# Attention scores: the low parts of the keys kept twice over, so that the second score product contracts 128 rows

## The chip, the cores and the metric

The kernel runs on one core of one Trainium2 chip. The metric is the device time of one launch in microseconds; before the change the median of three runs is 2069.76 us (2068.32 to 2070.65).

## What is computed

The reference is a network for one sequence of 512 tokens and a width of 1024, all in float32. A first block joins a pooling mixer with an attention of 8 heads of 64 columns over blocks of 256 keys (below: moba) and has a large MLP. A second block has two layers: one with differential attention (8 heads, each with two score maps of 64 columns; below: diff), one with windowed attention (16 query heads, 4 key heads, 64 columns; below: swa), each followed by a gated MLP with a small convolution. What bears on the change is the product that makes the scores, which all three attentions have:

```python
s_own = jnp.einsum('bhqd,bhkd->bhqk', qc, k_own) - slope * dist[None, None]      # moba
...
s = jnp.einsum('bqhd,bkhd->bhqk', qb, k).astype(jnp.float32) * scale             # diff
...
s = jnp.einsum('bnqhgd,bnchd->bnhgqc', q, kb).astype(jnp.float32) * (d ** -0.5)  # swa
```

## The kernel before, in words

TensorE multiplies in the type `float32r`, which keeps fewer bits than float32. Every operand is therefore held as a high part and a low part (`split`, line 75: ScalarE writes the high part, VectorE what is left over), and a linear layer makes three products of each pair of 128x128 weights and 128x512 activations (`mm3`, line 102: high by high at line 105, low by high at 106, high by low at 107). The weights come through `wst` (two buffers, loaded from SyncE's queue), and are split into `whi` and `wlo` (four buffers each, lines 93, 91 and 94).

Scores have a contraction of 64 only. Two heads (or the two maps of a diff head) share a tile of 128 partitions, head m = 0 in partitions 0 to 63 and m = 1 in 64 to 127. `stack_q` (line 810) rearranges a query tile by three copies so that each of the two heads has a full tile, with high parts in one half and low parts in the other. `stack_k` (line 817) likewise makes two tiles from the keys' high parts, each holding one head's high part twice. All these copies are DMAs from SBUF to SBUF on SyncE's queue. The score of a query block is then made by two products (`dots`, line 823): step 0 (line 827) contracts 128 rows, [query high; query low] with [key high; key high]; step 1 (line 830) contracts only the 64 partitions of head m, query high with key low, straight from the tile of the keys' low parts (`qkl` in moba, `dl` in diff, `kl` in swa). The query is the stationary operand, the keys stream.

In the program of a query block (`scores`, lines 585, 909 and 1095) these two products are followed by others into the same bank: in moba from the third query block on by one that contracts 2 rows (line 601, the gate's mask), and always by one for the distance (line 603); in swa by one for the band (line 1121); in diff by none, and there steps 0 of both maps are written down before steps 1 of both. The result is read by VectorE (a maximum: lines 605, 929 and 1123), ScalarE takes the exponential, and two to five query blocks later TensorE turns the weights (`flip`) and multiplies them with the values (`values`).

Attention is woven into linear work (`weave`, line 154): the generator `lin` makes queries, keys, values and part of the next projection, `att` the query blocks, and a table of stages and microseconds says how much linear work stands ahead of each block. A scheduler then orders the instructions of each engine when the program is built; at run time each engine works through its own order and waits on semaphores.

Of the kernel before, what the change touches and what calls it, by code (L numbers as in the profile page):

```python
# [15 lines left out]
S = 512  # L16
D = 1024
# [12 lines left out]
def f32(ap):  # L30
    return ap.bitcast(F32)


class Net:
# [16 lines left out]
    # ---------------------------------------------------------------- helpers  # L51
    def mm_ps(self, shape=(128, S)):
        """a bank for a linear layer's output: outside attention its banks are shared out too"""
        banks = (("mm", 2), ("sc", 2), ("mm", 2), ("sc", 2), ("pv", 1))[:self.wide]
        self.bank = (self.bank + 1) % len(banks)
        tag, bufs = banks[self.bank]
        return self.ps.tile(list(shape), F32, name=tag, tag=tag, bufs=bufs)
# [17 lines left out]
    def split(self, src, hi, lo, scale=None):  # L75
        """hi + lo = src (* scale)"""
# [32 lines left out]
    def tiles(self, w, k0, kt, cols):  # L109
        """weight tiles [128, kt, 128] (hi, lo) for the column starts in cols, loaded two at a time"""  # L110
# [12 lines left out]
    def linear_steps(self, w, x, cols, evac, k0=0, group=1, order=None, ready=None, first=None, ahead=(), hold=None):  # L123
        """a linear layer as a generator that yields after each k tile: ns of tensor time, or a mark it waits for;
        group output tiles (first, the first ones) take their k tiles in turn"""
# [28 lines left out]
    def weave(self, att, lin, pace):  # L154
        """attention chunks with linear work between them: pace gives (stage, us of linear work behind it by then)"""
# [4 lines left out]
        def advance():  # L160
            """one step of the linear work; None if it waits for a mark or has ended"""
# [43 lines left out]
    # -------------------------------------------------------------- constants  # L205
# [33 lines left out]
    def load_cols(self, names, rows):  # L239
        """per-channel columns of the rows of names"""  # L240
# [11 lines left out]
    def late_consts(self):  # L252
        nc, a = self.nc, self.a
        # rotary tables
# [36 lines left out]
    def conv_cols(self, rows):  # L291
        """conv columns: taps 0..2 and the bias, tile by tile"""
# [6 lines left out]
    # ------------------------------------------------------------------ norms  # L299
    def rsqrt(self, x, y, tmp):  # L300
        """y = x ** -0.5 for narrow tiles"""
# [7 lines left out]
    def col_stats(self, acc, which):  # L309
        """token-column sums [128, NT] of a feature-major tile, times the constant in self.ones"""  # L310
# [6 lines left out]
    def bcast(self, col):  # L317
        """[128, S] in PSUM, every partition the row of the token columns col [128, NT]"""
# [19 lines left out]
    def rstd(self, wide=True):  # L338
        """the token columns rstd [128, NT] and, wide, their broadcast over partitions [128, S]"""
# [13 lines left out]
    def later(self, f):  # L353
        """f's result, computed where it is first asked for"""
# [12 lines left out]
    def pre(self, n, src, gain, gi, fast=False):  # L367
        """squares and the gained split of tile n of the next layer's input"""
# [6 lines left out]
    # --------------------------------------------------------------- block one  # L375
    def load_x(self):
        """x, turned feature-major, with the first layer's first tiles on its heels"""
# [131 lines left out]
    def v_steps(self, w, c0, Rcol, dst, x):  # L509
        """token-major values: dst(t) -> (hi, lo) APs [128, 256] for the 256 columns from c0"""  # L510
# [14 lines left out]
    def moba(self, win, R, Rcol, P):  # L525
# [25 lines left out]
        def qk(i):  # L551
            def evac(n, ps):
# [3 lines left out]
                lo = P.tile([128, S], F32R, name="qkl%d" % n, tag="qkl%d" % n, bufs=2)  # L556
                self.split(f, hi, lo, 0.125 if n == 0 else None)
                sw = self.stacked(4 + i % 2 * 2 + n)
                QK[i, n] = (f, hi, sw, lo)
                if n == 0:  # L560
                    self.stack_q(hi, sw, lo)
                else:
                    self.stack_k(hi, sw)
# [10 lines left out]
        def gate(i):  # L574
            g = self.st_ps((2, 256))
            nc.tensor.matmul(g, QK[i, 2], QK[i, 0][0][:, 256:], start=True, stop=True)
            mr = P.tile([2, 256], F32, name="mr", tag="mr", bufs=2)
            nc.vector.tensor_scalar(mr, g, 0.125 / 256, NEG, op0=OP.mult, op1=OP.is_lt)
            mk = P.tile([2, 256], F32R, name="mk", tag="mk", bufs=2)
# [32 lines left out]
        def flip(h, t):  # L612
            """key block b, query block t of the transposed weights lies at 3 b + t"""
# [154 lines left out]
    def post(self, y, h, gain, gi, meanwhile):  # L768
        """the next layer's input from h + y * rstd of one operand, gained already, which ends in self.h"""
# [8 lines left out]
    # --------------------------------------------------------------- block two  # L778
    def rope(self, P, ps, cosR, sinR, hi, lo, scale=None):
        """split of the rotated tile: x * cos + swap(x) * sin, with the norm's rstd in the tables"""  # L780
# [12 lines left out]
    def spill(self):  # L793
        """h to DRAM: attention takes its tiles"""
# [14 lines left out]
    def stack_q(self, a, b, lo):  # L809
        """a = [hi 0; hi 1], lo = [lo 0; lo 1] -> a = [hi 0; lo 0], b = [lo 1; hi 1]"""  # L810
# [5 lines left out]
    def stack_k(self, a, b):  # L816
        """a = [hi 0; hi 1] -> a = [hi 0; hi 0], b = [hi 1; hi 1]"""
# [3 lines left out]
        nc.sync.dma_start(f32(a[64:, :]), f32(a[:64, :]))  # L821

    def dots(self, ps, q, k, m, qs, ks, step, last=False):
        """one of two products that make queries' dots with keys, of half m of the stacked tiles"""
        nc = self.nc
        if step == 0:
            nc.tensor.matmul(ps, q[m][:, qs], k[m][:, ks], start=True, stop=False)  # L827
        else:
            pp = slice(64 * m, 64 * m + 64)
            nc.tensor.matmul(ps, q[m][pp, qs], k[2][pp, ks], start=False, stop=last)  # L830

    def pv(self, ps, v, ph, pl, ps0, ph0, first, last):
        """values of 64 columns: v is [hi lo], and ps gets hi's products in its upper half, lo's in its lower;
        the first covers the bank"""
# [6 lines left out]
    def halves(self, P, ps, hi, lo):  # L841
        """split of the sum of the halves of pv's product"""
# [4 lines left out]
    def tables(self, P, R):  # L847
        nc = self.nc
        """the rotary tables times rstd; the sine's takes the place of R"""
# [9 lines left out]
    def diff(self):  # L859
# [4 lines left out]
        with tc.tile_pool(name="diff", bufs=1) as P:  # L864
# [31 lines left out]
            def qk(h):  # L896
                def evac(n, ps):
                    e = h % 2 * 4 + 2 * n
                    hi, sw = self.stacked(e), self.stacked(e + 1)
                    lo = P.tile([128, S], F32R, name="dl%d" % n, tag="dl%d" % n, bufs=2)  # L900
# [3 lines left out]
                    else:  # L904
                        self.stack_k(hi, sw)
# [565 lines left out]
```

## Time and profile before

| | |
|---|---|
| three runs | 2068.32, 2069.76, 2070.65 us |
| span of the profiled execution | 2068.3 us |
| TensorE (PE) busy | 2029.0 us, 98% |
| VectorE (DVE) busy | 1271.2 us, 61% |
| ScalarE (ACT) busy | 799.0 us, 39% |
| GpSimd (POOL) busy | 444.3 us, 21% |
| mean granted TensorE clock | 0.996 of 2.4 GHz |
| line 830 (the 64-row products) | 160 products: 32 in moba, 64 in diff, 64 in swa |
| moba's scores | from about 140 to 238 us of the span |
| diff's scores | from about 797 to 981 us |
| swa's scores | from about 1478 to 1598 us |

The profiled execution has no time of its own beside its span; the span equals the shortest of the three runs and lies 1.5 us under their median. In the trace a matmul's record begins when it starts and ends after its pipeline has drained, so the records of a dense stream overlap; what a product costs the stream is the distance from its start to the start of the next, not its duration. `PEld` is the load of the stationary operand, `SPq` SyncE's queue of DMA issues. A line such as `64*128 64x512` reads: 64 rows by 128 columns of the array used, a streamed operand of 64 partitions by 512 columns.

### The profile page before, as it was taken

Reading aid. Unit: us, or ns where it says so; the run is one execution under the profiler, and the core shown is the slowest. Engines: PE = TensorE matmul, PEld = TensorE weight load, DVE = VectorE, ACT = ScalarE, POOL = GpSimd, SP = SyncE. Lnnn points to the kernel's source line nnn. Section 1 sums busy time; section 2 is a strip of 40 time slices with the busy share of each in tenths; the row PEclk is TensorE's granted clock in tenths of the full one; section 3 lists DMA queues with packets and bytes.
Section 4 is the critical chain, followed back from the end, with each engine's and each line's share of the span. In section 5 each row is a group of like instructions: output and inputs, shape, how many; then the busy total and the mean of one; then the engine's idle time right before and its main releaser. Section 6 shows DMA issues by size and latency. Waiting matters only on the chain.

```text
span 2068.3 us, 25392 instructions
## 1 busy us (share of the span) xinstructions
PE 2029.0 (98%) x9426; PEld 1625.9 (79%) x9426; DVE 1271.2 (61%) x2038; ACT 799.0 (39%) x1388; POOL 444.3 (21%) x514
## 2 busy tenths in 40 slices
PE   8999999899999989999999999999999999999997
PEld 7887787787888877777788888887877788888886
DVE  6456655723444487778675465667688675465665
ACT  4324434422222354555343231334466343332342
POOL 5011224100000231110221113132234221113122
PEclk9999999999999999999999999999999999999999
DMA  5342344232332355433232332334532232334331
GB/s 195 98 139 57 100 147 138 90 102 82 102 102 93 111 159 139 110 90 103 83 88 94 107 101 84 92 127 143 145 92 70 82 102 88 96 102 126 88 102 61
DMA packets 260493, 218.82 MB, mean 106 GB/s; under 512 B 9285, under 2 KB 235666, under 8 KB 260370
## 3 DMA queue, kind: packets, MB, share of 16 engines
q1 hardware_dynamic: 256746, 211.90, 34.3%
q10 hardware_dynamic: 3624, 5.31, 0.8%
q8 instruction: 74, 1.21, 0.2%
q14 instruction: 49, 0.40, 0.1%
HBM read 182.83 MB, written 14.16 MB: 95 GB/s over the span
## 4 chain that ended last, share of the span: by engine, by line
PE 91%; DVE 6%; issue 1%; ACT 1%; DMA 1%; POOL 0%; SPq 0%; ACTq 0%; POOLq 0%; DVEq 0%
PE mm L105 12%; PE mm L107 12%; PE mm L106 12%; PE sc L106 10%; PE sc L107 10%; PE sc L105 10%; PE pv L105 5%; PE pv L107 5%; PE pv L106 5%; PE sc L830 3%; PE sc L827 2%; PE pv L839 1%; DVE ul L83 1%; PE tr L1148 1%; PE sc L1121 1%
## 5 line engine op out<-in xcount | busy, mean ns | idle before, releaser
L94 DVE TENSOR_TENSOR wlo<-wst,whi 128x1024 fp32r<-128x1024 f32 (+2 forms) x304 | 393.8, 1298 | 200.1 <-ACT whi L93 143.7
L93 ACT ACTIVATE whi<-wst 128x1024 fp32r<-128x1024 f32 (+2 forms) x203 | 207.2, 1025 | 459.6 <-PE sc L106 181.3
L106 PE MATMUL mm<-ul,whi 128*128 128x512 f32 x704 | 278.1, 395 | 11.5 <-DVE ul L83 11.5
L105 PE MATMUL mm<-uh,whi 128*128 128x512 f32 x704 | 281.4, 400 | 0.4 <-ACT uh L82 0.4
L107 PE MATMUL mm<-uh,wlo 128*128 128x512 f32 x704 | 276.7, 393 | 0.0
L91 POOL TENSOR_SCALAR whi<-wst 128x1024 fp32r<-128x1024 f32 (+2 forms) x101 | 108.0, 1069 | 734.0 <-PE mm L106 231.7
L105 PE MATMUL sc<-uh,whi 128*128 128x512 f32 x496 | 194.9, 393 | 0.0
L106 PE MATMUL sc<-ul,whi 128*128 128x512 f32 x496 | 194.3, 392 | 0.2 <-DVE ul L83 0.2
L107 PE MATMUL sc<-uh,wlo 128*128 128x512 f32 x496 | 194.2, 392 | 0.0
L106 PEld LDWEIGHTS mm<-ul,whi 128*128 128x128 f32 x704 | 132.8, 189 | 41.9 <-DVE ul L83 18.1
L105 PEld LDWEIGHTS mm<-uh,whi 128*128 128x128 f32 x704 | 132.7, 189 | 28.3 <-issue 3.5
L107 PEld LDWEIGHTS mm<-uh,wlo 128*128 128x128 f32 x704 | 132.5, 188 | 28.3 <-issue 1.7
L107 PEld LDWEIGHTS sc<-uh,wlo 128*128 128x128 f32 x496 | 93.5, 189 | 20.6 <-DVE wlo L94 0.7
L105 PEld LDWEIGHTS sc<-uh,whi 128*128 128x128 f32 x496 | 93.6, 189 | 19.6 <-issue 0.4
L106 PEld LDWEIGHTS sc<-ul,whi 128*128 128x128 f32 x496 | 93.6, 189 | 19.3 <-DVE ul L83 0.5
L105 PE MATMUL sc<-ah,whi 128*128 128x512 f32 x264 | 104.4, 396 | 0.0
L106 PE MATMUL sc<-al,whi 128*128 128x512 f32 x264 | 104.3, 395 | 0.0
L107 PE MATMUL sc<-ah,wlo 128*128 128x512 f32 x264 | 104.2, 395 | 0.0
L105 PE MATMUL pv<-uh,whi 128*128 128x512 f32 x256 | 100.7, 393 | 0.0
L107 PE MATMUL pv<-uh,wlo 128*128 128x512 f32 x256 | 100.6, 393 | 0.0
L106 PE MATMUL pv<-ul,whi 128*128 128x512 f32 x256 | 100.2, 391 | 0.0
L1233 ACT ACTIVATE cv<-cu,cc 128x512 f32<-128x512 f32 x88 | 71.0, 813 | 60.3 <-DVE cu L1231 60.2
(455 smaller groups left out, 4343.5 us busy)
## 6 DMA issues: line engine op xcount, KB each, us to landing
wst<-ffn_w_up SPq DMA_DIRECT2D x88, 512.0 KB
wst<-w_up SPq DMA_DIRECT2D x16, 1024.0 KB
wst<-w_down SPq DMA_DIRECT2D x16, 1024.0 KB
wst<-ffn_w_down SPq DMA_DIRECT2D x16, 1024.0 KB
wst<-w_in SPq DMA_DIRECT2D x16, 512.0 KB
wst<-w_in SPq DMA_DIRECT2D x8, 1024.0 KB
wst<-diff_w_qkv SPq DMA_DIRECT2D x16, 512.0 KB
wst<-ple_w_gate SPq DMA_DIRECT2D x8, 1024.0 KB
```

The source lines that it names most:

```text
L83: nc.vector.scalar_tensor_tensor(lo, src, scale, f32(hi), op0=OP.mult, op1=OP.subtract)
L91: nc.gpsimd.tensor_scalar(hi, src, 1.0, 1.0, op0=OP.mult, op1=OP.mult)
L93: nc.scalar.activation(hi, src, AF.Copy)
L94: nc.vector.tensor_tensor(lo, src, f32(hi), op=OP.subtract)
L105: nc.tensor.matmul(ps, ah, bh, start=first, stop=False)
L106: nc.tensor.matmul(ps, ah, bl, start=False, stop=False)
L107: nc.tensor.matmul(ps, al, bh, start=False, stop=last)
L827: nc.tensor.matmul(ps, q[m][:, qs], k[m][:, ks], start=True, stop=False)
L830: nc.tensor.matmul(ps, q[m][pp, qs], k[2][pp, ks], start=False, stop=last)
L839: nc.tensor.matmul(*args, start=first and x == 0, stop=last and x == 1)
L1121: nc.tensor.matmul(blk(sc)[:, m0:m1:2], identr, blk(band)[:, c + m0:c + m1:2], start=False, stop=True)
L1233: nc.scalar.activation(v, u[:, 1:S + 1], AF.Identity, bias=cc[:, 3, ft:ft + 1], scale=cc[:, 1, ft:ft + 1])
```

## The change

Step 1 of a score becomes a product of 128 rows, like step 0: the same stacked query tile, [high; low] in one order or the other, by a tile that holds the head's low key parts twice. The low parts are stacked by the same three copies as the high ones, in place (`lo`, for head 0) and into a new tile (`lw`, for head 1). There is one such pair for each key tile: 4 in moba, 8 in diff, 2 in swa, thus 42 more copies of 128 KB on SyncE's queue. The second product now also adds query low by key low, which was left out before. Room for the new tiles comes from single buffers where there were two: the low part of the queries (`qkl0`, `dl0`, `ql`) and the mask's two small tiles (`mr`, `mk`). In swa the first key tile's copy takes the free tile `h7`. Comments and docstrings go too; line numbers rise by two or three. The core of the diff:

```diff
@@ moba, qk @@
-                lo = P.tile([128, S], F32R, name="qkl%d" % n, tag="qkl%d" % n, bufs=2)
+                lo = P.tile([128, S], F32R, name="qkl%d" % n, tag="qkl%d" % n, bufs=n + 1)
                 self.split(f, hi, lo, 0.125 if n == 0 else None)
                 sw = self.stacked(4 + i % 2 * 2 + n)
-                QK[i, n] = (f, hi, sw, lo)
                 if n == 0:
+                    QK[i, n] = (f, hi, sw)
                     self.stack_q(hi, sw, lo)
                 else:
-                    self.stack_k(hi, sw)
+                    lw = P.tile([128, S], F32R, name="qkm", tag="qkm", bufs=2)
+                    QK[i, n] = (f, hi, sw, lo, lw)
+                    self.stack_k(hi, sw, lo, lw)
...
-            mr = P.tile([2, 256], F32, name="mr", tag="mr", bufs=2)
+            mr = P.tile([2, 256], F32, name="mr", tag="mr", bufs=1)
...
-    def stack_k(self, a, b):
+    def stack_k(self, a, b, *more):
         nc = self.nc
         nc.sync.dma_start(f32(b[64:, :]), f32(a[64:, :]))
         nc.sync.dma_start(f32(b[:64, :]), f32(a[64:, :]))
         nc.sync.dma_start(f32(a[64:, :]), f32(a[:64, :]))
+        if more:
+            self.stack_k(*more)

     def dots(self, ps, q, k, m, qs, ks, step, last=False):
-        nc = self.nc
-        if step == 0:
-            nc.tensor.matmul(ps, q[m][:, qs], k[m][:, ks], start=True, stop=False)
-        else:
-            pp = slice(64 * m, 64 * m + 64)
-            nc.tensor.matmul(ps, q[m][pp, qs], k[2][pp, ks], start=False, stop=last)
+        self.nc.tensor.matmul(ps, q[m][:, qs], k[2 * step + m][:, ks], start=step == 0, stop=last and step == 1)
...
@@ diff, qk @@
-                    lo = P.tile([128, S], F32R, name="dl%d" % n, tag="dl%d" % n, bufs=2)
+                    lo = P.tile([128, S], F32R, name="dl%d" % n, tag="dl%d" % n, bufs=n + 1)
...
-                        self.stack_k(hi, sw)
+                        lw = P.tile([128, S], F32R, name="dm", tag="dm", bufs=2)
+                        self.stack_k(hi, sw, lo, lw)
                         self.marks.add(("dqk", h))
-                    QK[h, n] = (hi, sw, lo)
+                    QK[h, n] = (hi, sw, lo, lw) if n else (hi, sw)
...
@@ swa, evac_k and q_steps @@
-                self.stack_k(hi, sw)
-                K.append((hi, sw, lo))
+                lw = P.tile([128, S], F32R, name="km") if n else self.stacked(7)
+                self.stack_k(hi, sw, lo, lw)
+                K.append((hi, sw, lo, lw))
...
-                    ql = P.tile([128, S], F32R, name="ql", tag="ql", bufs=2)
+                    ql = P.tile([128, S], F32R, name="ql", tag="ql", bufs=1)
```

The order of the instructions moves little, and at three kinds of place. First SyncE's queue in moba, at the keys of the first pair of heads (`qkh1` high part, `qkl1` low part, `st5` and `qkm` the second tiles, `wst` a weight load). Before:

```order
L819 DMA st5_1159<-qkh1_1155 64x512
L820 DMA st5_1159<-qkh1_1155 64x512
L116 DMA wst_1684<-w_in 128x8x128 x2
L821 DMA qkh1_1155<-qkh1_1155 64x512
L99 DMA wst_1951<-w_in 128x8x256
```

and with the change:

```order
L821 DMA st5_1159<-qkh1_1155 64x512
L822 DMA st5_1159<-qkh1_1155 64x512
L821 DMA qkm_1160<-qkl1_1156 64x512
L822 DMA qkm_1160<-qkl1_1156 64x512
L116 DMA wst_1696<-w_in 128x8x128
L823 DMA qkh1_1155<-qkh1_1155 64x512
L823 DMA qkl1_1156<-qkl1_1156 64x512
L116 DMA wst_1696<-w_in 128x8x128
L99 DMA wst_1967<-w_in 128x8x256
```

Three copies have come in, the third copies of the high and of the low part stand next to each other behind a weight load, and the other half of that load stands behind them.

Second TensorE's order in moba, where the second pair of heads has its first query block (`sc` the bank of the scores, `mm` a linear layer's, `tr` the turned weights of an earlier block). Before:

```order
L827 MATMUL sc_1566<-qkh1_1433,qkh0_1364 128x128
L830 MATMUL sc_1566<-qkl1_1434,qkh0_1364 128x128
L603 MATMUL sc_1566<-dist_946,si_1564 128x128
L105 MATMUL mm_1558<-uh1_137,whi_1452 128x512
L106 MATMUL mm_1558<-ul1_138,whi_1452 128x512
L107 MATMUL mm_1558<-uh1_137,wlo_1453 128x512
L619 MATMUL tr_1579<-ident_72,pr_1502 128x128 x3
```

and with the change:

```order
L830 MATMUL sc_1574<-qkh1_1437,qkh0_1368 128x128
L105 MATMUL mm_1566<-uh1_137,whi_1460 128x512
L106 MATMUL mm_1566<-ul1_138,whi_1460 128x512
L107 MATMUL mm_1566<-uh1_137,wlo_1461 128x512
L621 MATMUL tr_1587<-ident_72,pr_1510 128x128
L830 MATMUL sc_1574<-qkl1_1438,qkh0_1368 128x128
L605 MATMUL sc_1574<-dist_946,si_1572 128x128
L621 MATMUL tr_1587<-ident_72,pr_1510 128x128 x2
```

The second product of this block has moved behind three linear products and one transpose; no product is added or lost.

Third SyncE's queue at the end of diff, at the keys of the last head, where the loads that bring the residual tiles back (`h0` to `h7`) stand too. Before:

```order
L819 DMA st7_7978<-st6_7977 64x512
L820 DMA st7_7978<-st6_7977 64x512
L804 DMA h2_8241<-hs_5797 128x512
L804 DMA h0_8237<-hs_5795 128x512
L821 DMA st6_7977<-st6_7977 64x512
L804 DMA h1_8239<-hs_5796 128x512
```

and with the change:

```order
L821 DMA st7_8022<-st6_8021 64x512
L822 DMA st7_8022<-st6_8021 64x512
L821 DMA dm_8036<-dl1_8023 64x512
L822 DMA dm_8036<-dl1_8023 64x512
L806 DMA h0_8285<-hs_5811 128x512
L823 DMA st6_8021<-st6_8021 64x512
L806 DMA h1_8287<-hs_5812 128x512
L823 DMA dl1_8023<-dl1_8023 64x512
```

The last copy of the low part stands behind two of the residual loads.

## Rows read from the trace of the kernel before

**Rows 1.** The page: busy time of each engine, share of the span, instructions.
```profile
PE 2029.0 (98%) x9426; PEld 1625.9 (79%) x9426; DVE 1271.2 (61%) x2038; ACT 799.0 (39%) x1388; POOL 444.3 (21%) x514
```

**Rows 2.** Waits of TensorE: us in total, times, longest.
```profile
PE mm L106 <- DVE ul L83: 11.5, 14, 2.3
...
PE sc L827 <- ACT pr L932: 0.9, 3, 0.3
```

**Rows 3.** Idle time of the weight loads before line 830 in diff: us, times.
```profile
  issue: 16.2, 52
```

**Rows 4.** TensorE in order of time, diff: start us, us, then what it is.
```profile
852.51 0.40 PE L827 MATMUL sc<-st,st 128*128 128x512 f32 x1
852.84 0.50 PE L830 MATMUL sc<-dl,st 64*128 64x512 f32 x1
853.27 0.51 PE L107 MATMUL mm<-uh,wlo 128*128 128x512 f32 x1
853.62 0.39 PE L105 MATMUL mm<-uh,whi 128*128 128x512 f32 x1
...
854.07 0.39 PE L107 MATMUL mm<-uh,wlo 128*128 128x512 f32 x1
```

**Rows 5.** The same view where both maps' products stand side by side, the first of twelve.
```profile
797.01 0.63 PE L827 MATMUL sc<-st,st 128*128 128x512 f32 x2
797.57 0.50 PE L830 MATMUL sc<-dl,st 64*128 64x512 f32 x2
...
798.34 0.40 PE L106 MATMUL mm<-ul,whi 128*128 128x512 f32 x1
```

**Rows 6.** The same view in swa.
```profile
1526.03 0.34 PE L827 MATMUL sc<-st,st 128*128 128x384 f32 x1
1526.29 0.44 PE L830 MATMUL sc<-kl,st 64*128 64x384 f32 x1
1526.66 0.38 PE L1121 MATMUL sc<-band,identr 128*128 128x256 f32 x1
1526.88 0.40 PE L105 MATMUL mm<-uh,whi 128*128 128x512 f32 x1
```

**Rows 7.** The same view in moba, at a product of 2 rows.
```profile
180.88 0.38 PE L601 MATMUL sc<-sel,mk 2*128 2x256 f32 x1
181.19 0.50 PE L603 MATMUL sc<-dist,si 128*128 128x512 f32 x1
```

**Rows 8.** Stretches of moba, diff and swa: length, busy us of each engine, clock, DMA.
```profile
140.00:238.00 98.00, 98.00 (x458) 70.36 (x456) 64.23 (x150) 43.96 (x113) 19.48 (x36) 1.00 0.23 60
797.00:981.00 184.00, 182.88 (x992) 139.04 (x991) 151.37 (x331) 100.06 (x218) 24.49 (x18) 1.00 0.37 102
1478.00:1600.00 122.00, 121.77 (x614) 88.84 (x613) 100.76 (x297) 82.13 (x245) 47.23 (x81) 1.00 0.32 89
```

**Rows 9.** Waits of VectorE for TensorE, in the stretches of diff and of swa.
```profile
DVE st L929 <- PE sc L830: 12.8, 19, 3.7
...
DVE pr L1123 <- PE sc L1121: 5.3, 8, 1.4
```

**Rows 10.** Second key tile of moba: SyncE's issues, VectorE's low part, its first use.
```profile
160.81 0.60 SPq L820 DMA_DIRECT2D st<-qkh  x1
...
163.29 0.46 SPq L821 DMA_DIRECT2D qkh<-qkh  x1
...
161.46 0.68 DVE L80 TENSOR_TENSOR qkl<-qkf,qkh 128x512 fp32r<-128x512 f32 x1
...
170.65 0.32 PE L830 MATMUL sc<-qkl,qkh 64*128 64x128 f32 x1
```

**Rows 11.** The last head's keys in diff: the high part's last copy, first use.
```profile
963.04 0.47 SPq L821 DMA_DIRECT2D st<-st  x1
...
967.49 0.50 PE L830 MATMUL sc<-dl,st 64*128 64x512 f32 x2
```

**Rows 12.** Waits of SyncE's queue with a weight load: us in total, times, longest.
```profile
SPq L116 <- DVE wlo L94: 451.4, 46, 25.9
```

More of the change, by code (lines that the diff above doesn't have):

```diff
@@ L576, in gate @@
             nc.tensor.matmul(g, QK[i, 2], QK[i, 0][0][:, 256:], start=True, stop=True)
-            mr = P.tile([2, 256], F32, name="mr", tag="mr", bufs=2)
+            mr = P.tile([2, 256], F32, name="mr", tag="mr", bufs=1)
             nc.vector.tensor_scalar(mr, g, 0.125 / 256, NEG, op0=OP.mult, op1=OP.is_lt)
-            mk = P.tile([2, 256], F32R, name="mk", tag="mk", bufs=2)
+            mk = P.tile([2, 256], F32R, name="mk", tag="mk", bufs=1)
             nc.vector.tensor_scalar(mk, mr, NEG, None, op0=OP.mult)
```

## The prediction
> **What bounds the kernel now.** I read the page first: TensorE is busy for 2029.0 of 2068.3 us, 98% of the span, and no other engine passes 61% [rows 1]. The list of TensorE's waits says the same from the other side: the largest entry is 11.5 us, all in front of linear layers, and for scores there is 0.9 us [rows 2]. So a microsecond comes out of the time if it comes out of TensorE's stream and no other engine is about to take over in that stretch. But a busy TensorE need not be a dense one, so I read it in order of time. In a linear layer two products of 512 columns take 0.45 us from start to start (853.62 to 854.07 in [rows 4]); I round one to 0.23, and use shares of it for fewer columns. Around a 64-row product the stream opens: step 0 starts 0.33 us before it, it keeps the next product off for 0.43 us, and that one the product behind it for 0.35 us [rows 4]. Three products take 1.11 us, where 3 x 0.23 = 0.69 would do. The toll is 0.42 us, in three pieces of about 0.10, 0.20 and 0.12: the array goes from 128 rows to 64 and back, and empties both times. The list of the weight loads' idle time has the same mark: 52 times in diff the load of the 64-row product waited for nothing but "issue" [rows 3].
>
> **What the change removes.** One toll for each place where the row count changes. In diff there are 64 products in 52 places [rows 3], so 12 places hold two side by side, one map each. The 40 single ones cost 0.42 us: 16.8 us. In a double one the two products start together (one row stands for both), and five products and the next one's start span 797.01 to 798.34, 1.33 us [rows 5], against 5 x 0.23 = 1.15: 0.18 us, by 12 is 2.2 us. Diff: 19.0 us.
>
> In swa a score's three products run over 384, 384 and 256 columns and take from 1526.03 to 1526.88, 0.85 us [rows 6]; their 1024 columns are worth 0.46. That is 0.39 us by 64 products: 25.0 us. The narrower blocks have the same pieces.
>
> In moba 16 of the 32 blocks have no mask product and save some 0.40 us each, 6.4 us. In the other 16 a product of 2 rows follows. It has a toll of its own: 256 columns take 0.31 us to the next start [rows 7], where 0.12 would do. There the array still leaves the 128 rows once and comes back once, so only the 64-row product's own 0.20 us goes: 3.2 us. Moba: 9.6 us.
>
> The sum on TensorE is 53.6 us. The 128-row product itself is not dearer: in every row above what sets the distance is the number of streamed columns, and step 0 with 128 rows runs in the same place.
>
> **What it adds.** 42 copies, at about 0.5 us of SyncE's issue time each [rows 10]: 21 us on a queue that spends over 450 us waiting to get rid of one kind of weight load alone [rows 12]; nothing, while weights are that far ahead. The query's single buffers cost nothing: the copies that read a tile are long done when the next query tile is split, a head or a pair later in moba and diff.
>
> A later arrival is the real cost. A copy that overwrites the source of another is issued 2.5 us after it (160.81 to 163.29), so 2.5 us bounds a copy from above [rows 10]. The low part of that key tile is ready at 161.46 + 0.68 = 162.1; two copies are out by 163.2, the third at 165.7 and done at 168.2; its first use is at 170.65 [rows 10]. With tolls gone that use comes about 1 us earlier, so some 1.5 us of slack is left. The other key tiles of moba have as much, those of diff more. The exception is the last head of diff: the high part's last copy goes out at 963.04 and the first use is at 967.49 [rows 11], and the low part's third copy now stands behind one residual load more. I charge between 0 and 4 us there, and take 2, as the slack left of 4.4 us is about one copy.
>
> **What gives out next.** VectorE. In moba it is busy for 64.2 of 98 us; with 88 us left that is 73%, and I keep 9 of the 9.6 us [rows 8]. In diff it is busy for 151.4 of 184 us [rows 8]; with the whole gain 165 us are left, 92%. It is idle for 32.6 us now, 12.8 of which it waits for the very products that come earlier [rows 9]. So most of the gain fits, but not evenly: I keep 15 of 19.0 us, the 2 us of the last head included. In swa VectorE has 100.8 us of work in 122 us [rows 8]; the whole gain would leave 97 us, less than its work. Without any idle time it would allow 21 us. It is idle for 21.2 us, and only 5.3 of that for the scores [rows 9]; if the other 15.9 all stayed, the stretch would take 116.7 us and the gain would be 5. Between 5 and 21 I take 15, nearer to the upper end, since ScalarE and GpSimd, for which it also waits, are themselves let loose by an earlier TensorE.
>
> The sum is 9 + 15 + 15 = 39 us. The profiled span of 2068.3 becomes 2029.3; the median of the runs shown lies 1.5 us above that span, so I forecast 2030.8, say **2031 us**.
>
> **The rivals.** A difference of 0.2%, 4.1 us, is about what a measurement of this kernel can tell from no change.
>
> *VectorE doesn't bind.* Its work slides into the stretches behind the scores and TensorE keeps nearly all of 53.6 us: 2014 to 2021, middle 2017. For it: TensorE hardly ever waits in these stretches today [rows 2]. Against: in swa work is over 100 us and the gap left 97. Chance 0.18.
>
> *VectorE binds hard and copies come late.* In swa only 5 us are gained, in diff 8, in moba 6, as each first score of a pair waits a little: 19 us, 2051; it spans 2043 to 2060. For it: the second product of moba's second pair was already put behind other work in the new order, and the slack there is 1.5 us. Chance 0.12.
>
> *The toll isn't the rows'.* If the stream opened because a second product goes into the same bank, it would stay; and the 12 double places would lose what they have, two products in the time of one: 12 x 0.23 = 2.8 us, 2072.6, within 0.2%. Against it: three products into one bank follow each other at 0.23 us in every linear layer [rows 4], and a product of 2 rows has the same toll [rows 7]. Chance 0.04. The Trainium skill, in "TensorE: Matmul & The Clock Gate" under "Why this matters for your kernels", speaks for keeping 64 rows: small contractions in distinct row groups run concurrently. The trace agrees with that for two neighbours, which start together [rows 5], and shows what the rule leaves out, that the pair still takes 0.18 us more than full rows.
>
> *Slower: copies behind a blocked weight load.* In the new order the third copies of moba's first pair stand behind a weight load, and such a load has waited up to 25.9 us for its buffer [rows 12]. TensorE would then stand for 25.9 less some 8 us of slack, 18 us, in each of four places: 2031 + 72 = 2103; slower from the third place on (3 x 18 = 54 over the 39 gained). Against: a load stood before the high part's third copy already, and no score waits for a DMA [rows 2]. Chance 0.04.
>
> **How the numbers follow.** The forecast has 0.62, with 2024 to 2042 as its own range. The range takes in the second case's lower end at 2014 and most of the third, to 2048. Faster by over 0.2% are the first three cases, 0.92; the same 0.04; slower 0.04.
>
> **What would show it.** Right: line 830 has 320 products, none with 64 rows; 128-row steps 0 and 1 start 0.23 us apart and the idle "issue" entries are gone; diff's scores take about 169 us, swa's about 107, moba's about 89; TensorE now has waits for VectorE's and ScalarE's work in swa, and VectorE stands above 90% there. Wrong: tolls that stay, waits of TensorE for a DMA at first scores, or swa under 100 us.

## The result, and the profile after

| | before | after |
|---|---|---|
| median of the runs | 2070.2 us (2068.32 to 2071.04, 4 runs) | 2037.31 us (2036.43 to 2038.25, 4 runs) |
| ratio after to before | | 0.9839, 95% interval 0.9828 to 0.9851 |
| profiled span | 2068.3 us | 2034.6 us |

The change is worth 33 us; the forecast was 39 (2031 us, range 2014 to 2048). The page of the changed kernel, against [rows 1]: TensorE loses 42.5 us of busy time, the other engines keep theirs.

```profile
PE 1986.5 (98%) x9426; PEld 1623.4 (80%) x9426; DVE 1271.0 (62%) x2038; ACT 797.7 (39%) x1388; POOL 446.0 (22%) x514
```

**The tolls are gone.** TensorE in order of time (start us, us, what it is), where both maps of diff stand side by side, against [rows 5], and behind the dots at a score of swa, against [rows 6]:

```profile
788.45 0.62 PE L830 MATMUL sc<-st,st 128*128 128x512 f32 x2
788.91 0.40 PE L830 MATMUL sc<-dl,st 128*128 128x512 f32 x1
789.15 0.40 PE L830 MATMUL sc<-dm,st 128*128 128x512 f32 x1
789.39 0.40 PE L105 MATMUL mm<-uh,whi 128*128 128x512 f32 x1
789.62 0.39 PE L106 MATMUL mm<-ul,whi 128*128 128x512 f32 x1
...
1506.69 0.40 PE L106 MATMUL mm<-ul,whi 128*128 128x512 f32 x1
1507.12 0.62 PE L830 MATMUL sc<-st,qb 128*128 128x384 f32 x2
1507.57 0.28 PE L1123 MATMUL sc<-band,identr 128*128 128x256 f32 x1
1507.69 0.52 PE L830 MATMUL sc<-st,qb 128*128 128x384 f32 x2
```

Five products, up to the start of the next one, take 788.45 to 789.62, 1.17 us where there were 1.33. Line 830 is now both steps, and in diff a product starts 0.23 to 0.24 us after the last. A score of swa takes 1507.12 to 1507.69, 0.57 us where there were 0.85 (its columns are worth 0.46); but 1506.69 to 1507.12 is 0.43 us for one linear product that is worth 0.23: the weight load of the score behind it waited 0.46 us for ScalarE.

The idle time of TensorE and of its weight loads before line 830 (us, times) says what. The "issue" entry, 33.9 us in 124 places of the whole trace before (16.2 us in 52 of them in diff, [rows 3]), has shrunk to one place; ScalarE's exponentials, whose bank the next score wants, stand first:

```profile
  ACT pr L1127: 8.5, 19
  ACT pr L933: 5.4, 17
  DMA dl<-dl: 2.2, 2
...
  issue: 0.4, 1
```

**Where the 33 us are.** I took the first and the last start of a score product in each attention from the two traces:

| stretch | before, us | after, us | gain |
|---|---|---|---|
| up to moba's first score | 142.5 | 144.1 | -1.6 |
| moba's scores | 95.0 | 86.5 | 8.5 |
| from there to diff's first score | 559.5 | 557.9 | 1.6 |
| diff's scores | 183.2 | 167.6 | 15.6 |
| from there to swa's first score | 497.9 | 499.8 | -1.9 |
| swa's scores | 119.1 | 107.8 | 11.3 |
| the rest | 471.0 | 470.9 | 0.1 |

The first row's 1.6 us are not the change's: two kernels with the same code up to there, the change and the one below that moves swa's cosine product, have 144.1 and 142.0 us. Of diff's 15.6 us, 1.9 are lost again in the next row: from diff's first score to swa's first the gain is 13.7 us. The three stretches by engine (length, then busy us and instructions of TensorE, weight loads, VectorE, ScalarE, GpSimd; granted clock, DMA share, GB/s), against [rows 8]:

```profile
142.00:232.00 90.00, 90.00 (x458) 68.67 (x457) 64.28 (x150) 44.06 (x113) 20.64 (x36) 1.00 0.31 81
788.00:957.00 169.00, 166.30 (x983) 141.96 (x981) 149.46 (x329) 98.43 (x216) 24.82 (x18) 1.00 0.47 125
1455.80:1563.70 107.90, 102.53 (x597) 83.42 (x596) 100.28 (x289) 78.19 (x238) 48.12 (x79) 1.00 0.39 109
```

VectorE is at 71% in moba, 88% in diff and 93% in swa. Swa had 25.0 us of tolls in 119.1; without them TensorE alone would need 94.1. It takes 107.8, so 13.7 us are waits that were not there. They are spread over many small entries (swa; us in total, times, longest):

```profile
PEld sc L830 <- ACT pr L1127: 6.9, 16, 1.2
...
DVE pr L1125 <- PE sc L1123: 4.3, 5, 2.0
...
PEld tr L1150 <- POOL pr L1137: 2.3, 4, 0.9
PEld tr L1150 <- issue: 2.2, 5, 1.1
...
PEld pv L839 <- DVE Tl L80: 1.8, 4, 0.6
```

No row names VectorE as a large wait. But ScalarE's exponential of line 1127 is itself behind VectorE's maximum (line 1125), and the transposes wait for GpSimd's scaled weights, which wait for VectorE's reciprocals (line 1133, 25.9 us in 15 places). VectorE itself hardly waits: 61 maxima stand in this stretch, and only before 5 of them did it wait for the score, 4.3 us in all; before the others it was at other work. So the busy engine is seen here at the end of such chains, not in a large row of its own.

### The profile page after: what moved, and what is told of

Its sections match the earlier page's. It is cut to its first block, busy times and chain, and to the rows that moved or that the text cites. A ratio compares the mean times of both kernels' runs of the same rounds, so it can differ in the third digit from the quotient of the medians.

```text
span 2034.6 us, 25469 instructions
## 1 busy us (share of the span) xinstructions
PE 1986.5 (98%) x9426; PEld 1623.4 (80%) x9426; DVE 1271.0 (62%) x2038; ACT 797.7 (39%) x1388; POOL 446.0 (22%) x514
## 4 chain that ended last, share of the span: by engine, by line
PE 85%; DVE 8%; ACT 2%; issue 2%; DMA 2%; POOL 1%; SPq 1%; POOLq 0%; ACTq 0%; DVEq 0%
PE mm L105 11%; PE mm L107 11%; PE mm L106 11%; PE sc L107 10%; PE sc L105 10%; PE sc L106 10%; PE pv L105 5%; PE pv L106 5%; PE pv L107 5%; PE sc L830 2%; PE pv L839 1%; DVE ul L83 1%; DVE wlo L94 1%; PE st L313 1%; PE tr L950 0%
## 5 line engine op out<-in xcount | busy, mean ns | idle before, releaser
L106 PE MATMUL mm<-ul,whi 128*128 128x512 f32 x704 | 277.9, 395 | 11.3 <-DVE ul L83 11.3
```

The lines of the kernel that those rows point to most:

```text
L106: nc.tensor.matmul(ps, ah, bl, start=False, stop=False)
```

## The experiments

Edits are made to the changed kernel unless said otherwise. Times are medians; the runs of before, which a ratio compares with, have medians of 2068.78 to 2070.12 us.

### Whose is the gain: the rows' or the order's?

**All of the change, but step 1 with 64 rows again.**

```diff
+        pp = slice(64 * m, 64 * m + 64) if step else slice(128)
-        ... matmul(ps, q[m][:, qs], k[2 * step + m][:, ks], ...)
+        ... matmul(ps, q[m][pp, qs], k[2 * step + m][pp, ks], ...)
```

> The change with its copies and tiles, but the second score product takes 64 rows again. If the gain comes from the rows alone, all of it goes: 2068 to 2074 us against 2037 of the change and 2070 of before, and the tolls of 0.42 us around each 64-row product are back. If the stacking itself or the new order of the instructions gave part of the gain, the time lies clearly under 2066.

Measured: 2072.79 us (2071.87 to 2079.68, 10 runs), ratio 1.0018 (1.0008 to 1.0027). The whole gain goes, and the stages are as long as before: 95.0, 183.5 and 120.2 us. TensorE in order of time has [rows 4] again, 1.10 us for three products:

```profile
853.37 0.40 PE L831 MATMUL sc<-st,st 128*128 128x512 f32 x1
853.69 0.50 PE L831 MATMUL sc<-dm,st 64*128 64x512 f32 x1
854.12 0.51 PE L107 MATMUL mm<-uh,wlo 128*128 128x512 f32 x1
854.47 0.39 PE L105 MATMUL mm<-uh,whi 128*128 128x512 f32 x1
```

Operands, copies and buffers are those of the change here, and TensorE's order differs from the change's in 60 of 9426 places, all of them before swa; otherwise only the rows differ. So the toll is the rows', and what is left (copies, smaller buffers, another order) costs 3.0 us by the medians.

**128 rows, but the low parts not copied.**

```diff
-                    lw = P.tile([128, S], F32R, name="qkm", tag="qkm", bufs=2)
-                    QK[i, n] = (f, hi, sw, lo, lw)
-                    self.stack_k(hi, sw, lo, lw)
+                    QK[i, n] = (f, hi, sw, lo, lo)
+                    self.stack_k(hi, sw)
```

(and likewise in diff and swa)

> The second product takes 128 rows, but the low key parts are not copied: both heads read the tile as it was made, with the other head's low parts in its second half, so the scores' small correction is wrong; the 42 copies and the second tiles are left out. If the copies are hidden but for the last head of diff (one wait of TensorE of 1.0 us for the last copy, 1.9 us lost between diff's last score and its last transpose), 2034 to 2038 us. If the copies on SyncE's queue are why 33 us came and not 54, 2020 or less.

Measured: 2033.32 us (2033.06 to 2034.02, 4 runs), ratio 0.9826 (0.9809 to 0.9842): 4.0 us under the change, by the spans 3.2, and a little under the 2034 to 2038 that I expected. In the traces TensorE, VectorE, ScalarE and GpSimd have the order of the kernel before here, instruction by instruction. The change has another order in swa too, on all four engines, which the section on the change does not name among its places. So this run is the wider rows in the old order, 36.4 us under before, and the 4.0 are the copies together with the order that came with them.

Where they lie was not what I had priced. Swa's first score starts at 1456.5 us, in the change at 1455.8: up to there 36 of the 42 copies have cost nothing that this trace shows, the last head of diff included. The gain is in swa's stretch, 104.1 us instead of 107.8. VectorE is busy for 97.35 of it against 100.28, 94% of the one and 93% of the other. One way for the copies is seen at GpSimd's part of the rotation (`rs`), which needs copies (`rs<-rx`) that stand behind those of the low parts on SyncE's queue. GpSimd's waits for them in swa, in the change:

```profile
POOL rs L790 <- DMA rs<-rx: 15.2, 4, 11.5
```

and without the copies:

```profile
POOL rs L789 <- DMA rs<-rx: 1.9, 2, 1.0
```

The wait of 11.5 us ends after swa's first score, and GpSimd's product then meets one of VectorE's (the last section shows the two); VectorE also has seven cosine products in the scores' stretch instead of six. How much of the 4 us comes this way and how much by the order isn't told by this run.

**Moba's mask, 2 rows, widened to 128 with zeros.**

```diff
-        sel = P.tile([2, 2, 256], F32R, name="sel")
+        sel = P.tile([128, 2, 256], F32R, name="sel")
+        nc.gpsimd.memset(f32(sel), 0.0)
...
+        mk = P.tile([128, 256], F32R, name="mk")
+        nc.gpsimd.memset(f32(mk), 0.0)
-            mk = P.tile([2, 256], F32R, name="mk", tag="mk", bufs=1)
-            nc.vector.tensor_scalar(mk, mr, NEG, None, op0=OP.mult)
+            nc.vector.tensor_scalar(mk[0:2, :], mr, NEG, None, op0=OP.mult)
```

> The change, and moba's mask product takes 128 rows too, 126 of them zero. If the toll belongs to the change of the row count, each of 16 blocks loses what is left of it, 0.10 + 0.19 + 0.10 us: 6 us, 2030 to 2033, with moba's scores in about 80 us instead of 86.5, since VectorE works only 69 of 90 us there. If the toll belongs to 64-row products or to second products as such, no change: 2036 to 2039.

Measured: 2031.06 us (2030.75 to 2031.83, 4 runs), ratio 0.9815 (0.98 to 0.9829), 6.2 us under the change and **the fastest kernel of this study**. Moba's scores take 81.2 us, 5.3 less. TensorE in order of time, against [rows 7]:

```profile
177.30 0.44 PE L832 MATMUL sc<-qkh,qkh 128*128 128x512 f32 x1
177.58 0.39 PE L832 MATMUL sc<-qkl,qkh 128*128 128x512 f32 x1
177.81 0.28 PE L605 MATMUL sc<-sel,mk 128*128 128x256 f32 x1
177.92 0.39 PE L607 MATMUL sc<-dist,si 128*128 128x512 f32 x1
178.16 0.40 PE L105 MATMUL mm<-uh,whi 128*128 128x512 f32 x1
```

The next product starts 0.11 us after the mask's start, where it was 0.31, with the same 256 columns, and TensorE's order is the change's, instruction by instruction. This is another product and another row count, with other operands: with the 64-row run it settles that the toll belongs to the rows. That it is paid where the row count changes, and not once for each product, is read from [rows 5] alone: two 64-row products side by side cost 0.18 us, less than a single one. The Trainium skill, "TensorEngine Tiling (Array Packing)", "Key Properties", says that changing the tiling mode drains TensorE; these runs agree in that the stream opens around products of other rows and closes without them, though no trace shows the drain itself. Its price here is 0.42 us for a single 64-row product amid 128-row ones.

**Swa undone, moba and diff changed.**

```diff
+        if self.third and step:
+            pp = slice(64 * m, 64 * m + 64)
+            self.nc.tensor.matmul(ps, q[m][pp, qs], k[2][pp, ks], start=False, stop=last)
+            return
```

(and swa's keys stacked as before)

> The change in moba and diff alone: swa keeps its 64-row second products and has no copies of low key parts. By the stages of the two traces swa gave 11.3 us between its first and last score: 2047 to 2050 if the stages simply add up. If swa's 25 us of tolls had come out whole and been lost elsewhere, 2058 or more.

Measured: 2048.78 us (2047.95 to 2049.44, 4 runs), ratio 0.9901 (0.9886 to 0.9916). Swa's part of the gain is 2048.78 less 2037.31, 11.5 us, as in the table of stretches (11.3); by the distances from their own runs of before it is 12.9. The stages add up within 2 us. Swa's scores take 119.8 us with VectorE at 99.89 us of work, 83%: with the tolls it had room.

### What stands in swa's way?

**VectorE given more to do, in both kernels.** Three more passes over each rotated tile of swa, in before and in the change:

```diff
+        for _ in range(3 if self.third else 0):
+            nc.vector.scalar_tensor_tensor(x, x, 0.0, x, op0=OP.mult, op1=OP.add)
```

> The kernel before, and in swa each rotated query and key tile passes VectorE three times more (x = x times 0 plus x, the same values): about 0.7 us each, some 14 to 16 us more work for VectorE between swa's first and last score, outside the chain of the scores. If swa before is bound by TensorE and VectorE's idle 21 us can take it, 2070 to 2075. If every microsecond of VectorE already counts there, 2083 to 2086.

> The change with the same work added in swa. If VectorE's amount of work bounds swa with the change, nearly all of it is paid: 2048 to 2053. If swa with the change still has room on VectorE, 2037 to 2042, as little as the kernel before pays.

Measured: 2092.42 us for before (2091.54 to 2094.4, 4 runs), ratio 1.0105 (1.009 to 1.012); 2060.91 us for the change (2060.24 to 2063.46, 4 runs), ratio 0.9951 (0.9934 to 0.9967). Before pays 22 us and the change 24: both are above every range that I expected, and that before would absorb the work fell. But the pair doesn't decide between the theories either, since more than VectorE's work has moved. Swa's first score comes later (1483.0 us after 1478.1 in before, 1469.1 after 1455.8 in the change), linear work has left the stretch (from first to last score TensorE had 597 products in both kernels, and now has 571 and 534), and the granted clock, 1.00 in [rows 8], is 0.91 and 0.92 on the stretch's mean. I had added a cost to one engine and thereby changed the order that the scheduler writes: a doubled cost is a clean test only where the order stays.

**Less work for VectorE, three ways.** First its cosine product of swa given to GpSimd:

```diff
-        nc.vector.tensor_tensor(x, x, cosR, op=OP.mult)
+        (nc.gpsimd if self.third else nc.vector).tensor_tensor(x, x, cosR, op=OP.mult)
```

> The change, and in swa the product of a rotated tile with the cosine is made by GpSimd instead of VectorE: 6.7 us less work for VectorE between swa's first and last score, outside the chain of the scores. If VectorE's amount of work is what bounds swa now, swa's scores take 101 to 104 us instead of 107.9 and the time is 2030 to 2034. If the wait is the length of the chain score, maximum, exponential, transpose, not the amount of work, 2036 to 2040.

Measured: 2038.05 us (2037.37 to 2040.13, 4 runs), ratio 0.985 (0.9835 to 0.9864): no gain. VectorE's work from first to last score falls from 100.28 to 95.22 us, but it now waits for GpSimd in front of the next step of the same tile, and swa takes 111.1 us. The waits of VectorE:

```profile
DVE rx L792 <- POOL rx L791: 7.9, 7, 1.7
```

The work went away and came back as a wait, so this run says nothing on what VectorE's work is worth. The second leaves the product out:

```diff
-        nc.vector.tensor_tensor(x, x, cosR, op=OP.mult)
+        if not self.third:
+            nc.vector.tensor_tensor(x, x, cosR, op=OP.mult)
```

> The change, and in swa the product with the cosine is left out, so that the queries and keys there are rotated wrongly: 6.7 us less work for VectorE, with no new wait for GpSimd in its place, which took 7.9 us of VectorE's time when GpSimd made this product. If the amount of VectorE's work bounds swa, 3 to 7 us less: 2030 to 2034. If not, 2036 to 2039.

Measured: 2034.93 us (2033.63 to 2035.41, 4 runs), ratio 0.9825 (0.9811 to 0.984); 2.4 us under the change, which falls between the two ranges that I expected, and swa 104.9 us (-2.9). Behind swa's last score 1.4 us of this are lost again (472.3 us to the end instead of 470.9). The stretch by engine:

```profile
1454.90:1559.80 104.90, 99.76 (x595) 81.67 (x594) 97.47 (x289) 81.42 (x243) 47.47 (x82) 1.00 0.39 105
```

The cosine product was 6.7 us there, but VectorE's work falls by only 2.8: other work has moved in. The stretch is shorter by as much as the work that is left, and stands at 93% as in the change.

The third leaves swa's maximum out (the exponential is offset by the sink alone, and the sink's own exponential likewise):

```diff
-                nc.vector.tensor_scalar(p[:, :w_], sc, -1.0, nsink[:, h:h + 1], op0=OP.mult, op1=OP.min,
-                                        accum_out=st[:, 1, t:t + 1])
-                nc.scalar.activation(p[:, :w_], sc, AF.Exp, bias=st[:, 1, t:t + 1], accum_out=st[:, 2, t:t + 1])
+                nc.scalar.activation(p[:, :w_], sc, AF.Exp, bias=nsink[:, h:h + 1], accum_out=st[:, 2, t:t + 1])
```

> The change without swa's maximum over a block's scores: the exponential takes the sink alone as its offset, and VectorE's 61 passes over the scores, some 33 us of its 100 in this stretch, are left out. If VectorE bounds swa, TensorE becomes the bound again and swa's scores take 95 to 99 us instead of 107.9: 2025 to 2029. If something else holds it (ScalarE, the copies, the score banks' number), 2033 or more.

Measured: 2032.52 us (2031.53 to 2036.95, 4 runs), ratio 0.9819 (0.9804 to 0.9833); 4.8 us under the change, swa 101.4 us. The 95 to 99 that I expected were missed. VectorE is no longer the bound, and something else is, as swa's waits show:

```profile
1457.20:1558.70 101.50, 95.66 (x591) 81.36 (x591) 75.51 (x172) 79.86 (x245) 51.07 (x83) 1.00 0.42 116
```

```profile
POOL pr L1135 <- DVE st L1131: 33.1, 18, 3.8
...
PEld tr L1148 <- issue: 6.9, 8, 2.1
...
PE tr L1148 <- DVE st L1130: 3.7, 6, 1.7
```

VectorE is at 74%. The wait of the scores for the exponential falls from 6.9 us to 1.1; in its place the transposes wait, at the end of the chain exponential, sum, reciprocal, GpSimd's scaling. So with VectorE's 24.8 us gone, only 6.4 come out of swa, and 2.0 of these are lost again behind it: another limit lies close behind. The run takes away work of VectorE and a step of the chain from score to exponential at once, and doesn't tell the two apart.

**The other limit alone: transposes and values one block later.**

```diff
-                    if 0 <= g - 5 < 64:
-                        flip(*divmod(g - 5, 4))
+                    if 0 <= g - 6 < 64:
+                        flip(*divmod(g - 6, 4))
```

(the values likewise; to make room the weights' tiles in two sizes, four buffers each, and the tiles of the sums in two buffers instead of three)

> The change, and in swa a block's weights are turned and multiplied one block later (six blocks behind the score instead of five, with eight buffers for them instead of six); VectorE's work is the same. TensorE lost some 7.8 us in front of transposes in swa's stretch, beyond their own length. If that is the length of the chain from score to transpose, 3 to 7 us less: 2030 to 2034. If VectorE's amount of work is all that holds swa, the waits only move to the score banks: 2036 to 2039.

Measured: 2037.98 us (2035.69 to 2039.72, 4 runs), ratio 0.9848 (0.9834 to 0.9863): nothing. The stretch by engine:

```profile
1456.80:1563.80 107.00, 100.90 (x591) 82.31 (x590) 99.77 (x290) 78.25 (x238) 49.35 (x79) 1.00 0.38 109
```

VectorE is at 93% again. But the waits in front of the transposes have not gone: those of TensorE and of its weight loads together are 6.2 us in the change and 11.8 here. TensorE's largest there (us in total, times, longest) is now for VectorE's low parts, which free the transposes' banks, and was 0.4 us in the change:

```profile
PE tr L1150 <- DVE Tl L80: 3.5, 6, 0.9
```

So more distance to the transposes is worth nothing here, and what is waited for instead is in part again work of VectorE. That fits a bound by VectorE's amount of work. It doesn't prove it: the score banks, of which swa uses three, were not varied in any run, and a score's bank is held as long as VectorE's maximum and the exponential behind it take to come.

### A faster version still?

**The mask and the later transposes together**, and then also the sums of swa's weights once for each head and not for each two blocks (`if t == NT - 1: ts = slice(0, NT)`).

> The 128-row mask product of moba and the later transposes of swa together. If both gains stand and add, 2024 to 2028; if swa's is nothing, 2030 to 2032, as with the mask alone.

> The same, and swa's sums and reciprocals are made once for a head's four blocks instead of once for two: about 5 us less of VectorE's work and as much less of ScalarE's, but the first block's weights wait for the fourth block's sum. If VectorE's amount of work holds swa and six blocks are distance enough, 2 to 4 us under the version with the mask and the later transposes. If the chain to the transposes holds it, as much or more above it.

Measured: 2035.79 us (2032.41 to 2039.68, 4 runs), ratio 0.9833 (0.9817 to 0.985), and 2034.44 us (2031.97 to 2038.85, 4 runs), ratio 0.9834 (0.982 to 0.9849). Neither is under the mask alone (2031.06), and 1.4 us between the two is within the spread of either: the 2024 to 2028 that I expected of the first were missed, and on the sums the runs are inconclusive. The profile of the first is that of its slowest run, where swa takes 110.7 us at a mean granted clock of 0.98.

## Why the prediction was right, and where its sizes were off

**The toll and its price: right.** The removed 53.6 us were counted from [rows 3] to [rows 7]. In moba, where nothing binds, 8.5 us came of 9.6 priced and 9 kept; in diff 15.6 of 19.0 priced, 15 kept, of which 1.9 are lost again before swa. The 64-row run gives it all back, the run without copies has it in the order of before, and the mask run repeats it at another product. The rival that the toll isn't the rows' is refuted by these runs. The rival of concurrent row groups stood on a true sight, two 64-row products that start together [rows 5], and was answered by the next one: five products in 1.17 us instead of 1.33.

**Swa: the mis-sized term, 11.3 us instead of 15.** The step that failed is "between 5 and 21 I take 15, nearer to the upper end, since ScalarE and GpSimd ... are themselves let loose". It let VectorE's idle time shrink by 15 us, from 21.2 [rows 8] to 6 or so, and its work stay as it was. From first to last score VectorE was idle for 20.4 of 119.2 us before and is for 7.6 of 107.9 now: 12.8 us less, and its work has grown from 98.8 to 100.3 us. The 2.2 us that the idle time kept and the 1.5 of more work are the 3.7 that are missing. About 7 us of idle time stay in four kernels: 100.28 of 107.9 in the change, 97.47 of 104.9 without the cosine product, 99.77 of 107.0 with later transposes, 97.35 of 104.0 without the copies. That is 93 to 94%, a share that only these runs gave; had I divided the 98.8 us by 0.93, the stretch would have become 106.2 us and the gain 13.0. The upper end had VectorE at 100%.

That VectorE's amount of work is what holds swa is likely and not fully shown. For it speak that it waits for a score before only 5 of 61 maxima, and that the stretch shortens with its work in two runs (2.8 us less work and 2.9 less time without the cosine product, 2.9 and 3.7 without the copies). Open stays whether a fourth score bank would shorten the stretch with the same work. It is not shown either that 93% is its ceiling elsewhere.

**VectorE's own time also grew.** This I had not priced at all. Its operations of swa by shape (count, busy us, mean ns, idle before), of the change:

```profile
L791 DVE TENSOR_TENSOR rx<-rx,cosR 128x512 f32<-128x512 f32 x7 | 6.7, 962 | 0.0
L1132 DVE TENSOR_TENSOR st<-st 128x2 f32<-128x2 f32 x30 | 6.1, 205 | 0.7 <-ACT st L1131 0.2
L83 DVE SCALAR_TENSOR_TENSOR ql<-rx,st 128x512 fp32r<-128x512 f32 x7 | 5.9, 837 | 0.0
```

and of the kernel before:

```profile
L83 DVE SCALAR_TENSOR_TENSOR ql<-rx,st 128x512 fp32r<-128x512 f32 x7 | 4.9, 694 | 2.1 <-ACT st L82 1.9
...
L1130 DVE TENSOR_TENSOR st<-st 128x2 f32<-128x2 f32 x30 | 5.2, 172 | 1.6 <-ACT st L1129 1.2
...
L789 DVE TENSOR_TENSOR rx<-rx,cosR 128x512 f32<-128x512 f32 x6 | 4.6, 774 | 0.0
```

The same instructions are longer: 7 x (962 - 774) + 30 x (205 - 172) + 7 x (837 - 694) ns, 3.3 us. VectorE's busy time between first and last score rises by less, 1.5 us, since the records of neighbouring operations overlap more. The last section says what makes them longer.

**The copies: 2 us charged, 3 to 4 measured with the order that they bring, and elsewhere.** Charged was the last head of diff. Its wait is there, in order of time on TensorE:

```profile
947.03 0.60 PE L950 MATMUL tr<-ident,pr 128*128 128x128 f32 x4
948.62 0.50 PE L830 MATMUL sc<-dl,st 128*128 128x512 f32 x1 [0.99 <-DMA dl<-dl]
```

and on SyncE's queue:

```profile
940.74 0.59 SPq L822 DMA_DIRECT2D dm<-dl  x1
...
943.66 0.46 SPq L823 DMA_DIRECT2D dl<-dl  x1
```

The copy issued at 943.66 releases a product at 948.62, so it took up to 4.96 us, where I had bounded a copy by 2.5 [rows 10]; two residual loads stood ahead of it. Yet without copies the way from diff's first score to swa's is no shorter (668.1 us against 667.4). What copies and order cost is seen in swa, 3.2 us of span.

**The chain to the end.** By the first score of swa 22.3 us were gained, 24 forecast (9 + 15): 8.5 in moba and 13.7 from diff's first score to swa's. In swa 11.3, 15 forecast. With the 0.1 behind it that is the 33.7 us between the spans.

**The other rivals.** "VectorE doesn't bind" (2017) falls in swa and holds in moba. "VectorE binds hard and copies come late" (2051) had swa at 5, diff at 8, moba at 6, and each is too low. The range was said to take in most of this case, to 2048; it took in 5 of its 17 us, and not its middle. The slower one, copies behind a blocked weight load, has no trace: SyncE's queue waits as long as before [rows 12],

```profile
SPq L116 <- DVE wlo L94: 450.9, 46, 26.8
```

and the waits of scores for a low part's copy are the 2.2 us of the idle list above, weight load and product of the one place just shown. Of what the profile was to show, the 320 products of 128 rows, the distance of 0.23 us, the end of the "issue" entries and VectorE above 90% in swa came out. The lengths of the stages look right too (moba 89 forecast, 86.5 measured; diff 169, 167.6; swa 107, 107.8), but that is in part luck: the forecast's stretches before, 98, 184 and 122 us, are up to 3 us longer than the 95.0, 183.2 and 119.1 from first to last score, and in swa that covers most of the missing gain. Of the signs of being wrong one showed, small: the wait of 0.99 us for a DMA at the last head's first score.

## What to carry to other kernels

In a dense stream of TensorE, look for products whose row count differs from their neighbours', and price them by start-to-start distance, not by busy time: here 0.42 us for one such product, and filling its rows with useful or zero data takes it away, 33 us for three attentions and 6 more for a mask of 2 rows. Before the whole gain is credited, divide the next engine's work in that stretch by a share below one: here it reached 0.93, known only after the runs. And a test that adds work to an engine should leave the order of the others alone, or be read with that in mind.

## What the runs showed of the hardware

**VectorE and GpSimd hold each other up.** An operation of VectorE that overlaps one of GpSimd can last until that one has ended, or some tenths of a microsecond longer. Swa of the change, VectorE in order of time:

```profile
1458.36 1.45 DVE L791 TENSOR_TENSOR rx<-rx,cosR 128x512 f32<-128x512 f32 x1
...
1460.28 0.69 DVE L792 TENSOR_TENSOR rx<-rx,rs 128x512 f32<-128x512 f32 x1
...
1460.89 0.15 DVE L1132 TENSOR_TENSOR st<-st 128x2 f32<-128x2 f32 x1
...
1494.16 0.89 DVE L1132 TENSOR_TENSOR st<-st 128x2 f32<-128x2 f32 x1
```

and GpSimd:

```profile
1457.97 1.29 POOL L790 TENSOR_TENSOR rs<-rs,R 128x512 f32<-128x512 f32 x1 [11.53 <-DMA rs<-rx]
...
1493.76 1.29 POOL L790 TENSOR_TENSOR rs<-rs,R 128x512 f32<-128x512 f32 x1 [1.74 <-DMA rs<-rx]
```

GpSimd's products end at 1459.26 and 1495.05. The cosine product ends at 1459.81, 0.55 us later, the tiny 128x2 one at 1495.05, to the hundredth; alone they take 0.69 and 0.15 us. The Trainium skill, "SBUF — State Buffer", "SBUF: two separate sides", says that a VectorE operation with two SBUF inputs and a GpSimd operation that reads SBUF take a shared pair of ports in turn, each for its whole length; these rows agree. It was read from the traces, not tested by a run of its own. In swa of both traces the operations of the three shapes above that overlap no GpSimd record are all short (0.68 to 0.69 us for the cosine product, 0.69 for the low part, 0.14 to 0.16 for the sum); every longer one overlaps such a record, and some that overlap are short too. Between first and last score VectorE's records overlap GpSimd's, summed over operations, for 43.0 us before and for 53.2 us in the change: that is where the 3.3 us above come from.

**A copy of 128 KB from SBUF to SBUF behind two residual loads** took up to 4.96 us from its issue to the product that waited for it, twice the 2.5 that bounded one elsewhere [rows 10].

**The granted clock** of TensorE fell in the two kernels with more work for VectorE, after slices in which TensorE had gaps. Of the change with that work (length, TensorE's busy us, granted clock, DMA share, GB/s):

```profile
1545.00:1550.00 5.00, 2.23 (x10) 0.82 0.35 96
1550.00:1555.00 5.00, 5.00 (x22) 0.50 0.10 23
```

The second slice is at the lower level, 1.2 GHz, behind one in which the records cover 2.23 of 5 us and the mean has already fallen to 0.82; in swa's stretch of the change itself it is 1.00.
